# The instruction orders of a two-layer decoder kernel, chosen by another model of the framework

## The chip, the cores and the metric

The kernel runs on one core of a Trainium2 chip. The metric is the time of one execution on the device, in microseconds (us); the times given are medians of several executions. A core has engines that work side by side, each through its own list of instructions in order: PE (matmuls; PEld is its loading of weights), DVE (vector operations), ACT (activations, casts and copies), POOL, and SP, which here only issues DMAs (transfers between the device's memory and the core's own memory). An instruction that needs the result of another engine waits for it, and everything behind it on its own engine waits too.

## The reference

Two decoder layers on one sequence of 512 positions and 2048 features, in float32. Layer A is differential attention with 8 heads (two score matrices per head, values 256 wide), layer B forgetting attention with 16 heads on keys, values and forget gates that are projected once from layer A's result.

```python
for l in range(DEPTH):                                   # DEPTH = 2
    mod = c_act @ w_mod[l] + b_mod[l]                    # c_act = silu(c)
    shift, scale, gate = jnp.split(mod, 3, axis=-1)
    h = x * (1.0 + scale[:, None]) + shift[:, None]
    if l < N_A:                                          # layer A
        y = diff_attention(h, a_w_in[l], a_w_out[l], ...)
    else:                                                # layer B
        k_sh, v_sh, F_sh = shared_kv(x, c_act, kv_w_mod, kv_b_mod, kv_w, kv_b_f)
        y = forgetting_attention(h, b_w_in[l - N_A], b_w_out[l - N_A], k_sh, v_sh, F_sh)
    x = layer_norm(DN_ALPHA * x + gate[:, None] * y, ln_g[l], ln_b[l])
```

In `diff_attention`, a head's weights are softmax of its first scores less lambda times softmax of its second; the head's output is normalised by its root mean square and multiplied by `silu(g)`, before `w_out`.

## The kernel before

**Products in three parts.** Every float32 operand of a large product is split into a high part (a cast, on ACT) and a low part (the rest, on DVE), and `products` (L171) issues three matmuls: high by high, high by low, low by high. A weight tile covers 256 rows and 512 columns. `WeightStream` (L50) takes it through three steps: SP loads it (`wst`, four buffers, L46), ACT casts it (`whi`, three buffers, L93), DVE subtracts (`wlo`, three buffers, L94). For the 512 positions and one weight tile, `group` (L306) issues 24 matmuls (2 rows of tiles, 4 accumulators, 3 products).

**Stages.** The start computes layer A's shift and scale and the projections of the first two heads; its `sms` loads feed sums `sacc` on DVE (L474 to L476), which PE turns into columns (L506). Its steps follow a string (`START`, L30), and `tc.manual_schedule(engines={ET.DVE})` (L417) keeps DVE's instructions there in program order. Then layer A goes by heads: a group for values and gate (`vg[h]`, evacuated by `evac_vg`, where L675 makes `sg`) and a group for queries and keys (`qk[h]`), while the attention of the head before, cut into pieces, is put between the bursts of matmuls (`tick`, L290). A piece list ends with the tail of a head: `turn` (transposes of the weights, L720, split into `ah` and `al`), `values` (`o`, L736), `norm` (a copy and squares on ACT, L746 and L749, then sums, an inverse root and `og` on DVE, L750 to L755) and `store` (transposes of `og`, L767, and `ogT` on ACT, L769). There is one accumulator bank for `o` and one for transposes (`tr`); four for `acc`. After layer A come its output projection, the shared values and keys (`vj`, `kj`), eight pairs of heads of layer B, whose weights are turned at L1163 and split at L1166 and L1167, and the second output projection, which closes with the layer norm.

**Modulation in the background.** The other vectors of shift, scale and gate are products of one row with a matrix and are computed on DVE: `mod_stream` (L355) loads rows of the matrix (`ms`, L369) and adds them into `macc` (L384, L386). In layer A a load is 512 KB and there are two buffers; the second stream, during the projection of values and keys, has 256 KB and three. The next load into a buffer is issued when the `macc` that read it is done. A finished sum is split, summed over partitions by PE (L406, L407), and sent away (`mrow`, L408).

**What sets the order.** The program names its instructions in one sequence. The framework then sets the order in which each engine gets its own: it goes through the instructions with a model of how long each takes and takes, on each engine, an instruction that the model has ready first, so that the order on an engine may differ from the sequence. This is done for PE, ACT, DVE, SP and POOL, save DVE in the start. The model used is a simple one of the framework's own. On PE, 46 runs of instructions (440 instructions) stand outside the program's sequence.

## Time and profile before

| what | value |
|---|---|
| time, median of 3 executions | 2016.16 us (2014.56 to 2017.47) |
| time of the profiled execution | 2017.03 us |
| its span, first to last instruction | 2015.2 us |
| PE busy | 1966.7 us (98%) |
| DVE busy | 1334.4 us (66%) |
| ACT busy | 722.3 us (36%) |
| granted clock of PE, mean | 0.995 |
| moved by DMA | 353.79 MB, 176 GB/s on the mean |

The span is the profiler's; the time holds 1.8 us around it. In the page, a group of instructions is written as line, engine, operation, output<-inputs, count, then busy time and mean duration in ns, then the idle time of the engine ahead of it and what ended that. In the view of waits, a row is the waiting instruction, the one waited for, the total in us, how many times, and the longest. Lines are those of the kernel before; a line can be a helper's.

### The profile page before, as it was taken

What the parts mean: (1) busy time and instruction counts of PE and PEld (TensorE: products, weight loads), DVE (VectorE), ACT (ScalarE), POOL (GpSimd) and SP (SyncE); (2) the same over time, 40 slices, a digit from 0 to 9 for tenths busy, and PEclk for the clock granted to TensorE, in tenths of its full rate; (3) what the DMA queues carried; (4) which work ended last, traced back from release to release, by engine and by line L of the source; (5) the groups of instructions that cost most, each with busy time, mean ns of one, the idle gap of its engine ahead of it and who ended that gap; (6) DMA issues with size and microseconds to landing.
All of it is one profiled execution on the core that took longest, in us unless ns stands there. A gap on an engine that the chain in (4) does not pass through costs nothing.

```text
span 2015.2 us, 25053 instructions
## 1 busy us (share of the span) xinstructions
PE 1966.7 (98%) x9115; PEld 1624.6 (81%) x9115; DVE 1334.4 (66%) x2435; ACT 722.3 (36%) x1230; POOL 2.2 (0%) x10
## 2 busy tenths in 40 slices
PE   5999999999999999999999999999999999999997
PEld 4888878888878888888878877888888888888885
DVE  7887878777667677753575666645455555576678
ACT  2423444433333334432273222224333333453232
POOL 0000000000000000000000000000000000000000
PEclk8999999999999999999999999999999999999998
DMA  9995755574556565552344878844233323333754
GB/s 342 346 314 149 238 174 162 166 222 156 190 166 210 160 225 178 162 165 94 115 144 135 268 252 260 259 123 129 90 104 95 104 90 104 95 117 93 259 191 177
DMA packets 263095, 353.79 MB, mean 176 GB/s; under 512 B 18022, under 2 KB 162556, under 8 KB 262204
## 3 DMA queue, kind: packets, MB, share of 16 engines
q1 hardware_dynamic: 260592, 347.99, 53.7%
q10 hardware_dynamic: 2380, 4.21, 0.6%
q8 instruction: 71, 1.16, 0.2%
q14 instruction: 52, 0.43, 0.1%
HBM read 339.47 MB, written 12.66 MB: 175 GB/s over the span
## 4 chain that ended last, share of the span: by engine, by line
PE 77%; DVE 10%; DMA 10%; issue 2%; ACT 1%; SPq 1%; DVEq 0%; ACTq 0%
PE acc L173 22%; PE acc L175 22%; PE acc L174 22%; DMA ms<-in_w_mod_dram 7%; DVE macc L386 3%; DVE wlo L94 2%; PE sc L173 2%; PE sc L174 2%; PE sc L175 1%; DMA ms<-in_kv_w_mod_dram 1%; PE o L175 1%; PE o L174 1%; PE o L173 1%; PE tr L1163 1%; DMA sms<-in_w_mod_dram 1%
## 5 line engine op out<-in xcount | busy, mean ns | idle before, releaser
L93 ACT CAST whi<-wst 128x1024 fp32r<-128x1024 f32 (+2 forms) x339 | 349.5, 1032 | 672.9 <-PE acc L175 281.6
L94 DVE TENSOR_TENSOR wlo<-wst,whi 128x1024 fp32r<-128x1024 f32 (+2 forms) x339 | 404.4, 1195 | 268.1 <-ACT whi L93 263.9
L173 PE MATMUL acc<-whi,hh 128*128 128x512 f32 x1252 | 492.6, 397 | 0.9 <-ACT hh L933 0.8
L174 PE MATMUL acc<-wlo,hh 128*128 128x512 f32 x1252 | 489.7, 391 | 2.6 <-DVE wlo L94 2.6
L175 PE MATMUL acc<-whi,hl 128*128 128x512 f32 x1252 | 488.1, 390 | 0.0
L173 PE MATMUL acc<-hh,whi 128*128 128x512 f32 x1184 | 468.5, 396 | 1.3 <-ACT vt L977 0.9
L175 PE MATMUL acc<-hh,wlo 128*128 128x512 f32 x1184 | 462.3, 390 | 2.0 <-DVE wlo L94 2.0
L174 PE MATMUL acc<-hl,whi 128*128 128x512 f32 x1184 | 461.7, 390 | 0.0
L386 DVE SCALAR_TENSOR_TENSOR macc<-ms,cact,macc 128x512 f32<-128x512 f32 x360 | 269.9, 750 | 128.4 <-DMA ms<-in_w_mod_dram 95.6
L175 PEld LDWEIGHTS acc<-whi,hl 128*128 128x128 f32 x1252 | 235.3, 188 | 50.8 <-DVE hl L934 0.3
L174 PEld LDWEIGHTS acc<-wlo,hh 128*128 128x128 f32 x1252 | 235.6, 188 | 47.8 <-DVE wlo L94 4.3
L173 PEld LDWEIGHTS acc<-whi,hh 128*128 128x128 f32 x1252 | 235.7, 188 | 46.8 <-ACT hh L933 1.2
L175 PEld LDWEIGHTS acc<-hh,wlo 128*128 128x128 f32 x1184 | 222.3, 188 | 52.2 <-DVE wlo L94 4.2
L173 PEld LDWEIGHTS acc<-hh,whi 128*128 128x128 f32 x1184 | 222.5, 188 | 45.7 <-ACT vt L977 1.7
L174 PEld LDWEIGHTS acc<-hl,whi 128*128 128x128 f32 x1184 | 222.6, 188 | 41.1
L476 DVE SCALAR_TENSOR_TENSOR sacc<-sms,cact,sacc 128x512 f32<-128x512 f32 (+1 forms) x127 | 89.5, 705 | 4.8 <-DMA sms<-in_w_mod_dram 1.2
L1152 ACT ACTIVATE eb<-eb,mnb 128x128 f32<-128x128 f32 (+1 forms) x64 | 36.1, 563 | 96.4 <-DVE mnb L1149 95.2
L703 ACT ACTIVATE e<-e,mn 128x128 f32<-128x128 f32 (+3 forms) x64 | 36.0, 563 | 89.5 <-DVE mn L699 88.7
L1149 DVE CUSTOM_DVE_ANT_0 eb<-sc,biasb 128x128 f32<-128x128 f32 (+1 forms) x64 | 31.3, 490 | 52.7 <-PE sc L175 52.7
L1167 DVE TENSOR_TENSOR pTl<-tr,pTh 128x128 fp32r<-128x128 f32 (+1 forms) x64 | 31.2, 487 | 26.5 <-ACT pTh L1166 26.2
L1166 ACT CAST pTh<-tr 128x128 fp32r<-128x128 f32 (+1 forms) x64 | 27.2, 424 | 43.6 <-PE tr L1163 43.1
L769 ACT ACTIVATE ogT<-tr,subg 128x128 f32<-128x128 f32 x64 | 20.0, 364 | 56.4 <-PE tr L767 56.4
(251 smaller groups left out, 1739.2 us busy)
## 6 DMA issues: line engine op xcount, KB each, us to landing
wst<-in_a_w_in_dram SPq DMA_DIRECT2D x240, 256.0 KB
ms<-in_w_mod_dram SPq DMA_DIRECT2D x64, 512.0 KB
ms<-in_kv_w_mod_dram SPq DMA_DIRECT2D x64, 512.0 KB
wst<-in_kv_w_dram SPq DMA_DIRECT2D x64, 512.0 KB
ms<-in_w_mod_dram SPq DMA_DIRECT2D x128, 256.0 KB
wst<-in_b_w_in_dram SPq DMA_DIRECT2D x128, 256.0 KB
sms<-in_w_mod_dram SPq DMA_DIRECT2D x56, 512.0 KB
wst<-in_b_w_out_dram SPq DMA_DIRECT2D x48, 512.0 KB
```

Of the source, the lines that this page charges most:

```text
L93: self.nc.scalar.copy(hi[:, :, :w], st[:, :, :w])
L94: self.nc.vector.tensor_tensor(lo[:, :, :w], st[:, :, :w], hi[:, :, :w].bitcast(F32), op=ALU.subtract)
L173: PE.matmul(dst, lhs[0], rhs[0], start=start, stop=False)
L174: PE.matmul(dst, lhs[0], rhs[1], start=False, stop=False)
L175: PE.matmul(dst, lhs[1], rhs[0], start=False, stop=stop)
L386: V.scalar_tensor_tensor(acc, w, cact[:, kt : kt + 1], acc, op0=ALU.mult, op1=ALU.add)
L476: V.scalar_tensor_tensor(acc, w, sc, acc, op0=ALU.mult, op1=ALU.add)
L703: S.activation(e[:, :w], e[:, :w], AF.Exp, bias=mn, scale=-1.0, accum_out=rs)
L1149: V.tensor_tensor_reduce(out=e[:, :w], in0=sc[:, :w], in1=bias[:, :w], scale=-1.0, scalar=3.0e38, op0=ALU.add, op1=ALU.min, accum_out=mn)
L1152: S.activation(e[:, :w], e[:, :w], AF.Exp, bias=mn, scale=-1.0, accum_out=rs)
L1166: S.copy(pTh[:, 0 : i + 1, ts], src)
L1167: V.tensor_tensor(pTl[:, 0 : i + 1, ts], src, pTh[:, 0 : i + 1, ts].bitcast(F32), op=ALU.subtract)
```

## The change

`schedule_with_timeline_sim=True` is given to the framework's `TileContext`, by way of a small class that keeps the kernel's call as it was. With it, the pass that sets the orders takes its times from the framework's timeline simulator and not from the simpler model. The instructions themselves, their tiles and their buffers stay; nine lines are added ahead of the kernel, so that every line number of the kernel grows by 9.

```diff
-import concourse.tile as tile
+from concourse.tile import TileContext
 from concourse import mybir
...
+class tile:
+
+
+    @staticmethod
+    def TileContext(nc):
+        return TileContext(nc, schedule_with_timeline_sim=True)
+
...
 def tile_yoco(
     ctx: ExitStack,
-    tc: tile.TileContext,
+    tc: TileContext,
```

The set of instructions is the same on every engine (9068 matmuls and transposes on PE, 2437 instructions on DVE, 1095 on ACT, 1026 on SP, 15 on POOL). On PE, 369 runs of instructions (3134 instructions) now stand outside the program's sequence.

## The prediction

> **What bounds the kernel now.** I read the page's engine totals first, then PE's waits, then busy time by stretch, and after that single stretches of the timeline.

> ```profile
> span 2015.2 us, 25053 instructions
> ...
> PE 1966.7 (98%) x9115; PEld 1624.6 (81%) x9115; DVE 1334.4 (66%) x2435; ACT 722.3 (36%) x1230; POOL 2.2 (0%) x10
> ...
> L386 DVE SCALAR_TENSOR_TENSOR macc<-ms,cact,macc 128x512 f32<-128x512 f32 x360 | 269.9, 750 | 128.4 <-DMA ms<-in_w_mod_dram 95.6
> ```

> ```profile
> PE tr L506 <- DVE sacc L476: 11.4, 2, 11.0
> PE tr L767 <- DVE og L753: 4.4, 5, 1.3
> ...
> PE acc L174 <- DVE wlo L94: 2.6, 4, 1.0
> PE acc L175 <- DVE wlo L94: 2.0, 4, 0.9
> PE tr L767 <- DVE al L169: 0.9, 1, 0.9
> ...
> PE tr L720 <- DVE ss L750: 0.6, 1, 0.6
> ```

> ```profile
> 0.00:30.00 30.00, 13.37 (x67) 11.38 (x67) 19.25 (x41) 4.82 (x6) 1.60 (x9) 0.97 0.98 314
> 30.00:40.00 10.00, 7.41 (x22) 5.70 (x23) 6.94 (x11) 3.23 (x4) 0.00 (x0) 0.57 1.09 385
> ...
> 1100.00:1320.00 220.00, 214.81 (x934) 174.18 (x933) 143.32 (x179) 54.86 (x65) 0.00 (x0) 1.00 0.78 252
> 1320.00:1800.00 480.00, 480.00 (x2268) 399.47 (x2268) 269.07 (x527) 189.87 (x330) 0.00 (x0) 1.00 0.32 101
> ...
> 1950.00:2015.00 65.00, 51.20 (x224) 41.34 (x222) 55.82 (x98) 17.04 (x19) 0.00 (x0) 0.92 0.51 177
> ```

> PE's matmuls are the bound: 1966.7 of 2015.2 us. The columns of the last view are length, busy time of PE, PEld, DVE, ACT and POOL, the granted clock, the share of the DMA engines and GB/s. Of the 48.5 us in which PE is idle, 30.0 − 13.37 + 10.0 − 7.41 = 19.2 lie in the first 40 us and 65.0 − 51.20 = 13.8 at the end. Some 15.5 us are left for all the rest, and from 1320 to 1800 there is none. The instructions stay the same ones; only their order on PE, ACT, DVE and SP changes. So the most that a better order can give between 40 and 1950 us is 15.5 us, while a worse one can cost without limit: each engine takes its instructions in order, and PE stops wherever the order brings a matmul before its operand. I therefore set the new order beside the old one, instruction by instruction, and for each PE instruction that needs a result of ACT or DVE I counted the PE work that stands between the instruction that starts that result and the one that needs it. I call this the lead. Where the lead is shorter than the chain takes in the trace of before, the difference is a stall. 6343 of the 9068 matmuls and transposes change places (by up to 202), 1774 of 2437 on DVE, 692 of 1095 on ACT, 653 of 1026 on SP (by up to 16). The hand-written start keeps DVE's order alone.

> **Start: +2.5 us.**

> ```profile
> 33.82 0.94 SPq L425 DMA_DIRECT2D xt<-in_x_dram  x1
> 34.86 12.48 SPq L449 DMA_DIRECT2D sms<-in_w_mod_dram  x8
> 47.44 1.85 SPq L46 DMA_DIRECT2D wst<-in_a_w_in_dram  x2
> ```

> ```profile
> 41.38 1.02 PE L506 MATMUL tr<-ones,sacc 128*128 128x1 f32 x8 [0.37 <-DVE sacc L476]
> ```

> The new SP order puts this 1 MB `xt` load and these two 256 KB `wst` loads ahead of the `sms` loads of the next columns. At the 385 GB/s of 30 to 40 us, 1.5 MB take 4 us, and the sums on DVE that L506 waits for have no slack (0.37 us idle). A later `wst` costs nothing here: it is earlier now. Bounds 0 (later loads of `sms` are ahead again by as much) and 5; I take the middle.

> **First modulation stream, 190 to 276 us: +5.** Here the 512 KB `ms` loads have two buffers. The `macc` steps (L386) stand about six `wlo` splits (L94) earlier on DVE than before; a split behind a `macc` that waits for its load makes `acc` late. Bounds 0 and 10 (two to three loads late, priced below), middle taken.

> **Tails of the heads in layer A: +47, the largest term.** A head's last work is a chain: `turn` (L720), `ah`/`al` (L168/169), `o` (L736), the norm (L746 to L755), `tr` (L767), `ogT` (L769). Before, PE has weight products between its links. This is its price, in heads 2 to 3 (PE, then ACT, then DVE):

> ```profile
> 379.57 0.28 PE L175 MATMUL o<-vh,al 128*128 128x256 f32 x1
> 379.69 0.40 PE L173 MATMUL acc<-whi,hh 128*128 128x512 f32 x1
> 379.92 0.40 PE L174 MATMUL acc<-wlo,hh 128*128 128x512 f32 x1
> ...
> 386.51 0.38 PE L767 MATMUL tr<-ident,og 128*128 128x128 f32 x2
> ```

> ```profile
> 375.98 0.58 ACT L168 CAST ah<-tr 128x512 fp32r<-128x512 f32 x1
> ...
> 379.89 0.59 ACT L746 COPY og<-o 128x512 f32<-128x512 f32 x1 [0.80 <-PE o L175]
> ...
> 387.22 0.64 ACT L769 ACTIVATE ogT<-tr,subg 128x128 f32<-128x128 f32 x2
> ```

> ```profile
> 377.25 0.68 DVE L169 TENSOR_TENSOR al<-tr,ah 128x512 fp32r<-128x512 f32 x1
> ...
> 381.52 0.17 DVE L750 TENSOR_SCALAR ss<-ss 128x2 f32<-128x2 f32 x1 [3.59 <-ACT o L749]
> ...
> 383.98 0.88 DVE L753 SCALAR_TENSOR_TENSOR og<-og,rstd,sg 128x256 f32<-128x256 f32 x2
> ```

> The last `o` is done about 379.85; `og` is done at 384.86, some 4.6 to 5.0 us later, of which ACT's copy and squares are 1.6. PE filled these with 512-column products, 0.23 us each, and came to L767 only at 386.51: a lead of 6.8 us. The split after a transpose costs 0.58 + 0.68, about 1.3 us; `ogT`, which frees the one `tr` bank, 0.65. In the new order PE first issues all `acc` products of the group, and then this, with nothing between (the lead in us stands behind each):

> ```
> turn(0) 3.4, o 0.0, turn(1), o 0.0, turn(2), o 0.0, store(0) 1.1, turn(3) 0.0, o 0.0, store(1) 0.3, o x10, store(2) 0.0, acc of qk[3] 0.2
> ```

> The first `acc` of the next group needs `sg` (L675), which stands on DVE behind `og`. By the links: splits 0.8 + 1.0 + 1.6 (the third meets the squares of the norm, since there is one `o` bank), the rest of the first norm 1.9, `ogT` and the fourth split 0.65 + 1.3, the second norm 4.6, less 0.2 of lead: 11.6 us. On DVE more stands inside this chain:

> ```profile
> 354.81 0.75 DVE L386 SCALAR_TENSOR_TENSOR macc<-ms,cact,macc 128x512 f32<-128x512 f32 x1 [1.66 <-DMA ms<-in_kv_w_mod_dram]
> ...
> 363.11 0.75 DVE L386 SCALAR_TENSOR_TENSOR macc<-ms,cact,macc 128x512 f32<-128x512 f32 x1 [1.27 <-DMA ms<-in_kv_w_mod_dram]
> ```

> Six loads of two `macc` each stand between the first split and the first `og`, behind a `wlo` whose buffer PE frees only at the end of its `acc` products. The rows show the first `macc` of the third and of the fifth: 8.3 us for two loads, 4.15 each. With two buffers, two of the six can have landed, and the other four come in two pairs: 4.15 for the load and 1.5 for its `macc` (2 x 750 ns), twice, make 11.3; with `ogT` and the fourth split (1.95) and the second norm (4.6) about 18 us. The others, in order of time (new order beside the rows above): heads 3 to 4 a norm less 0.4, 4.2, and with four loads inside one such pair more (5.65 + 4.6), about 10.5; 4 to 5 a split and a norm, 5.9; 5 to 6 a norm and `ogT`'s turn, 4.9; 6 to 7 part of a norm and an `ogT`, 2.8, and 6.5 with the `macc` and `wlo` inside; 7 to the output projection a split, a norm, two `ogT` and the `hh` split, 7.5. Sum 53, by the links alone 37. Before's own stalls at these places go: 4.4 + 0.9 + 0.6 = 5.9 in the waits above. That leaves +47 with the loads and +31 without; I take 47, since the loads stand in the order that DVE has to follow. Bounds 31 and 60.

> **Second modulation stream, 1100 to 1317 us: +14.**

> ```profile
> DVE macc L386 <- DMA ms<-in_w_mod_dram: 72.5, 49, 3.6
> ```

> ```profile
> L369 SPq DMA_DIRECT2D ms<-in_w_mod_dram x127: 327/328/1771, 1096.4 to 1311.4; - x127
> ```

> ```profile
> 1295.58 1.22 DVE L94 TENSOR_TENSOR wlo<-wst,whi 128x1024 fp32r<-128x1024 f32 x1
> ...
> 1315.94 0.75 DVE L386 SCALAR_TENSOR_TENSOR macc<-ms,cact,macc 128x512 f32<-128x512 f32 x1
> ```

> 127 loads take 215 us, one in 1.71 us: with three buffers, each is issued when a `macc` ends, and DVE waits 72.5 us for them. This pace does not depend on the order. The new order sets each `wlo` behind more of these `macc`: the one that ran at 1295.58 now stands behind the one that ran at 1315.94, 12 further on. Counted in `wlo`, the last `macc` have 212 of them ahead and not 215. Three weight pairs are 3 × 24 products × 0.227 = 16.3 us of PE work, of which the `wlo` had 1 to 3 us to spare (PE waited up to 1.0 us for it, four times at each of two lines). So PE ends the stream 14 us later, and there is nothing behind it that makes this good, as PE is full to 1800. Bounds 8 (a spare of one and a half pairs) and 18.

> **End of layer B, 1845 to 1870 us: +5.5.** Four of the splits of `pTh`/`pTl` (L1166, L1167) and the `hh` split of the last heads follow their transposes with leads of 0 to 0.7; at the 1.3 us of a 512-column split, less what is narrower. Bounds 2 and 8.

> **The clock: +5.**

> ```profile
> 29.00:34.00 5.00, 1.41 (x5) 1.01 (x6) 2.45 (x5) 1.85 (x3) 0.00 (x0) 0.50 1.10 378
> 34.00:38.00 4.00, 4.00 (x10) 3.13 (x10) 3.54 (x5) 0.33 (x2) 0.00 (x0) 0.50 1.09 386
> ...
> 39.00:40.00 1.00, 1.00 (x6) 0.81 (x5) 0.96 (x2) 0.04 (x1) 0.00 (x0) 1.00 1.05 407
> ```

> Around 29 to 34 us PE has little to do, and the granted clock is half until past 38, although from 34 on PE is full: some 4.8 us of products at half speed, 2.4 us lost. The tails leave gaps of 4 us and more at six places. I take two such losses; bounds 0 and 14 (six). [...]

> **Gains: −2.** From 1400 to 1800 us the leads grow a great deal, but there PE has nothing to gain (480.00 of 480.00). Of the rest, some stalls between 248 and 273 us go. Bounds 0 and −7.5, all that is left of 15.5 after the 5.9 above and 2 that stay.

> **Sum.** 2.5 + 5 + 47 + 14 + 5.5 + 5 − 2 = +77. The profiled execution took 2017.0 us (its span and 1.8 us around it), 0.9 above the median of the three runs, 2016.2. So the forecast is 2093 us for a median. All low ends together give 0 + 0 + 31 + 8 + 2 + 0 − 7.5 = +33.5, 2050; the high ones 5 + 10 + 60 + 18 + 8 + 14 = +115, 2131. The prices are of one kind and can all be off in one direction, so the range is 2040 to 2140.

> **The rivals.**
> - The loads have landed when the tails come (links only, and `wlo` keeps its spare): 31 + 8 and the rest at their middle, without the clock, +50, 2066 us. For it: DVE is busy for only 66% of the span. Against: two buffers hold two loads, and more than two stand inside two of the chains.
> - All six gaps drop the clock: +9 on the sum, 2102; with the high ends 2131. For it: the stretch at 29 us. Against: it is one place, and the weak stretch there was longer than 4.6 us.
> - Faster: the longer leads outside the tails take away the 15.5 us of stalls in the middle, about 2004 us; with only half of it 2009. It would need the tail's chain to lie beside products after all, and the point at which that decides is a lead of about 4.6 us between the last `o` and its L767. Before has 6.8 there and the new order 0.0, so PE would have to come late to that place for another reason, and then time is lost already.
> - The change does nothing: excluded, since the orders differ; only an order that differs where PE has slack everywhere would give 2016.

> **How the numbers follow.** My sum with its loads inside (2075 to 2115) 0.5; links only 0.25; all clock drops or high ends 0.15; not slower 0.10, of which faster 0.07 and within 0.2% 0.03. About 0.2% (4 us) is what a measurement of this kernel can tell from no change. From 2040 to 2140 leaves out the not slower and a little beyond the top, under 2 in 10. Slower: 0.90.

> **What would show it.** Right: PE's waits of the changed kernel list L767's transposes on `og` and the next group's `acc` on `sg` (now lines 776 and 684) with some 30 us or more; PE's busy share in 300 to 900 us falls to about 93%; DVE waits for `ms` within the tails; the last `macc` of the second stream comes before the same number of `acc`, with PE waiting for `wlo` (line 103) 10 us and more; the granted clock shows stretches of 0.5 at tails. Wrong: a PE without gaps at 380 to 400, and `macc` that end ahead of the tails. I would be most wrong if PE's idle time were not at the tails but shared out over the whole of layer A, which would mean that leads are not what counts.

## The result, and the profile after

The changed kernel takes 2157.35 us (median; 2153.30 to 2159.07), the kernel before 2016.82 in the same series: a ratio of 1.0691, 95% interval 1.0667 to 1.0715. That is 140 us slower, where 2093 us had been forecast, in a range up to 2140. The sign was right, the size was not. The profiled execution has a span of 2155.3 us and a mean granted clock of 0.968.

The page of the changed kernel (its line numbers are 9 above those of before):

```profile
span 2155.3 us, 25058 instructions
...
PE 2011.1 (93%) x9115; PEld 1653.6 (77%) x9115; DVE 1327.8 (62%) x2435; ACT 716.0 (33%) x1230; POOL 2.1 (0%) x10
...
PEclk9999999799898999998999999999999999999998
```

Its PE waits (total, times, longest):

```profile
PE tr L776 <- DVE og L762: 48.6, 7, 12.7
PE tr L515 <- DVE sacc L485: 13.7, 2, 11.1
PE acc L184 <- DVE wlo L103: 9.5, 7, 3.5
PE acc L183 <- DVE wlo L103: 6.6, 4, 4.4
```

And busy time by stretch (length, busy PE, PEld, DVE, ACT, POOL, granted clock, DMA share, GB/s):

```profile
40.00:200.00 160.00, 145.46 (x667) 118.45 (x665) 117.73 (x165) 53.16 (x72) 0.56 (x1) 0.96 0.76 257
...
300.00:600.00 300.00, 265.54 (x1200) 217.78 (x1200) 184.42 (x400) 98.75 (x210) 0.00 (x0) 0.91 0.47 149
600.00:900.00 300.00, 275.00 (x1258) 227.36 (x1257) 189.83 (x394) 97.28 (x200) 0.00 (x0) 0.95 0.52 165
...
1320.00:1400.00 80.00, 71.37 (x295) 56.43 (x294) 49.54 (x64) 18.05 (x22) 0.00 (x0) 0.96 0.74 240
1400.00:1800.00 400.00, 396.32 (x1841) 329.35 (x1840) 207.64 (x383) 143.16 (x236) 0.00 (x0) 1.00 0.34 109
```

PE is idle for 2155.3 − 2011.1 = 144.2 us, 95.7 more than before. The other 44.4 us are in its busy time: the same matmuls took longer, in good part at a lower granted clock (0.968 in the mean and not 0.995), as the clock row shows. The transposes L776 wait 48.6 us for `og` where they waited 4.4, and `wlo` costs 16.1 us where it cost 4.6. Those are the places that the prediction named. Its sign for them, a busy share of about 93% from 300 to 900 us, came out as 88.5% and 91.7%; of the other waits that it named, those of the next group's `acc` for `sg`, there is only 0.6 us.

To see where the time came from, I gave each matmul its time at full clock and asked of both traces when PE has done the same amount of this work. The lateness of the changed kernel grows so:

```
stage (time before, us)              forecast   measured
start, 0 to 94                           2.5        4.6
94 to 218 (forecast: 190 to 276)         5         19.5
218 to 377                              -2         -5.8
tails of layer A, 377 to 909        47 + 5         92.7
909 to 1166                              0          1.6
second modulation stream, to 1325       14         16.0
layer B, to 1785                         0         -0.2
end of layer B, to 1908                  5.5        7.2
second output projection and end         0          4.5
sum                                     77        140.1
```

The 5 is the clock, which the forecast did not divide among the stages. Four terms lie within their bounds. Two do not: the tails, off by 41 us, and 94 to 218 us, off by 14.5. Of the 19.5 us there, 17 had arisen by 190 us, ahead of the stretch that the forecast named.

**A tail of layer A.** The last `o` of head 2 and the next transposes, on PE, ACT and DVE of the changed kernel:

```profile
427.52 0.41 PE L184 MATMUL o<-vh,al 128*128 128x256 f32 x1
434.01 0.66 PE L776 MATMUL tr<-ident,og 128*128 128x128 f32 x2 [6.08 <-DVE og L762]
434.77 0.80 PE L182 MATMUL acc<-hh,whi 128*128 128x512 f32 x1
```

```profile
427.97 0.59 ACT L755 COPY og<-o 128x512 f32<-128x512 f32 x1 [1.51 <-PE o L184]
428.45 1.21 ACT L177 CAST vh<-acc 128x256 fp32r<-128x256 f32 x4
429.51 0.43 ACT L758 ACTIVATE o<-o 128x256 f32<-128x256 f32 x1
...
429.90 0.69 ACT L683 ACTIVATE th<-acc 128x256 f32<-128x256 f32 x2
430.43 0.43 ACT L758 ACTIVATE o<-o 128x256 f32<-128x256 f32 x1
```

```profile
428.87 1.42 DVE L178 TENSOR_TENSOR vl<-acc,vh 128x256 fp32r<-128x256 f32 x4 [3.81 <-ACT vh L177]
431.01 0.17 DVE L759 TENSOR_SCALAR ss<-ss 128x2 f32<-128x2 f32 x1 [0.72 <-ACT o L758]
...
433.38 0.88 DVE L762 SCALAR_TENSOR_TENSOR og<-og,rstd,sg 128x256 f32<-128x256 f32 x2
```

PE does nothing for 6.08 us. The norm was priced at 4.6 from the rows of before; here four casts `vh` and two `th` stand on ACT between the copy and the last square, so that copy and squares take 2.9 us (427.97 to 430.86) and not 1.6. Four `vl` stand on DVE ahead of `ss` too, but are done before the last square. At heads 3 to 4, `macc` stand inside the norm too:

```profile
545.58 0.75 DVE L395 SCALAR_TENSOR_TENSOR macc<-ms,cact,macc 128x512 f32<-128x512 f32 x1 [1.25 <-DMA ms<-in_kv_w_mod_dram]
...
548.27 0.75 DVE L395 SCALAR_TENSOR_TENSOR macc<-ms,cact,macc 128x512 f32<-128x512 f32 x1 [1.09 <-DMA ms<-in_kv_w_mod_dram]
```

```profile
550.36 0.66 PE L776 MATMUL tr<-ident,og 128*128 128x128 f32 x2 [12.65 <-DVE og L762]
```

Only 1.25 + 1.09 of the 12.65 us are waits for loads; eight `macc` between `ss` and `og`, the first a shorter one, are another 5.7 (0.48 + 7 x 0.75). The gaps of the six tails, in order, are 20.6 (in ten pieces), 12.7, 10.1, 6.1, 8.5 and 8.5 us: 66.4 where 53 had been forecast, and each of the six is longer than its forecast.

**The clock.** Behind the tail above:

```profile
428.00:434.00 6.00, 0.00 (x0) 0.02 (x1) 4.03 (x19) 2.98 (x11) 0.00 (x0) 0.50 0.00 0
434.00:437.00 3.00, 2.89 (x7) 2.10 (x8) 1.77 (x5) 1.17 (x4) 0.00 (x0) 0.50 0.02 5
437.00:441.00 4.00, 4.00 (x12) 3.06 (x11) 0.00 (x0) 0.00 (x0) 0.00 (x0) 0.56 0.00 0
441.00:443.00 2.00, 2.00 (x11) 1.65 (x10) 0.00 (x0) 0.63 (x2) 0.00 (x0) 1.00 0.00 0
```

PE is full again from 434, at half speed until about 440 (12 matmuls in 4 us, then 11 in 2). The clock had been at half since about 407 us, through all the gaps between the pieces of this tail. The trace shows 15 such stretches of work at half speed between 44 and 1393 us, in 11 falls of the clock, with 27.6 us lost by the measure above, 1.8 for each stretch; 18 of it at the tails. These are the six tails (the granted clock is the third number from the right):

```profile
400.00:443.00 43.00, 22.35 (x79) 16.68 (x78) 24.31 (x66) 10.87 (x33) 0.00 (x0) 0.60 0.38 119
530.00:560.00 30.00, 17.23 (x73) 13.48 (x72) 19.52 (x43) 7.94 (x23) 0.00 (x0) 0.72 0.46 142
648.00:672.00 24.00, 13.78 (x55) 10.66 (x54) 11.58 (x30) 6.96 (x21) 0.00 (x0) 0.72 0.31 102
760.00:778.00 18.00, 11.73 (x51) 9.40 (x51) 7.02 (x24) 5.88 (x19) 0.00 (x0) 0.81 0.19 60
868.00:888.00 20.00, 11.49 (x47) 8.67 (x46) 14.35 (x36) 6.76 (x21) 0.00 (x0) 0.74 0.48 150
970.00:1000.00 30.00, 21.51 (x85) 16.01 (x84) 14.22 (x35) 8.11 (x20) 0.00 (x0) 0.77 0.53 154
```

### The profile page after: what moved, and what is told of

It reads as the page before. It is cut to its first block, busy times and chain, and to the rows that moved or that the text cites. A ratio compares the mean times of both kernels' runs of the same rounds, so it can differ in the third digit from the quotient of the medians.

```text
span 2155.3 us, 25058 instructions
## 1 busy us (share of the span) xinstructions
PE 2011.1 (93%) x9115; PEld 1653.6 (77%) x9115; DVE 1327.8 (62%) x2435; ACT 716.0 (33%) x1230; POOL 2.1 (0%) x10
## 4 chain that ended last, share of the span: by engine, by line
PE 73%; DMA 13%; DVE 9%; issue 2%; ACT 2%; SPq 1%; DVEq 0%; ACTq 0%
PE acc L182 21%; PE acc L183 20%; PE acc L184 20%; DMA ms<-in_w_mod_dram 8%; DMA ms<-in_kv_w_mod_dram 3%; DVE macc L395 3%; DVE wlo L103 2%; PE sc L182 2%; PE sc L184 2%; PE sc L183 2%; PE o L184 1%; PE o L182 1%; PE o L183 1%; PE tr L1172 1%; DMA sms<-in_w_mod_dram 1%
## 5 line engine op out<-in xcount | busy, mean ns | idle before, releaser
L182 PE MATMUL acc<-whi,hh 128*128 128x512 f32 x1252 | 480.9, 397 | 3.8 <-ACT hh L177 1.8
L184 PE MATMUL acc<-whi,hl 128*128 128x512 f32 x1252 | 480.8, 392 | 0.0
L183 PE MATMUL acc<-hl,whi 128*128 128x512 f32 x1184 | 468.7, 396 | 0.0
L776 PE MATMUL tr<-ident,og 128*128 128x128 f32 x64 | 15.2, 326 | 53.8 <-DVE og L762 48.6
L776 PEld LDWEIGHTS tr<-ident,og 128*128 128x128 f32 x64 | 8.8, 160 | 59.9 <-issue 51.1
```

The costliest lines, as they stand in the source:

```text
L182: PE.matmul(dst, lhs[0], rhs[0], start=start, stop=False)
L183: PE.matmul(dst, lhs[0], rhs[1], start=False, stop=False)
L184: PE.matmul(dst, lhs[1], rhs[0], start=False, stop=stop)
L776: PE.transpose(pt[:, e * P : (e + 1) * P], og[:, i % 2, e * P : (e + 1) * P], ident)
```

## The experiments

Time is that of the kernel named; the kernel before took 2014.9 to 2019.0 us in these series. Lateness is against the kernel before, by the measure above.

**Whose order: PE's or DVE's.** First by the program's own sequence in layer A. `a_pe` is this diff; `a_dve` has `ET.DVE`:

```diff
+    hand0 = ExitStack()
+    hand0.enter_context(tc.manual_schedule(engines={ET.PE}))
     load_parameters()
...
+    hand0.close()
     npool, n, nstats = zp
```

> The changed kernel with PE's instructions of layer A, from the second head to the output projection, kept in the program's sequence; DVE, ACT and SP stay with the new model. Theory 1 (the cost of layer A is PE's order: the tails stand bare): the 92 us by which PE falls behind over the six boundaries go, 2157 becomes 2055 to 2080. Rival (it is DVE's order, with loads inside the norm, whatever PE does): PE still waits for og, no more than 30 us come back, 2125 or more.

> The changed kernel with DVE's instructions of layer A kept in the program's sequence; PE, ACT and SP stay with the new model. Theory 1: the tails stay bare on PE and still cost about 6 us of norm each, only the loads inside go: 20 to 30 us less than 2157, 2127 to 2137. Rival (DVE's order is the cause): 60 us or more less, below 2097.

`a_pe` took 2131.3 us, the rival's number, and `a_dve` 2176.7, which neither gave. In `a_pe` the tails from heads 2 to 3 on add 33 us and not 92, as theory 1 has it, but the first heads add 28 us more than in the changed kernel. I put that down to the other engines' orders, which the new model set around another order of PE; no run shows it. In `a_dve`, 38 us arise at the last tail alone. The program's sequence is not the old order, so I held engines to the very order of the kernel before, by edges that only fix who is issued first (`PE_ORDER_OF_BEFORE` stands here for the packed list of names):

```diff
+def pin(tc, packed):
...
+    order = zlib.decompress(base64.b64decode(packed)).decode().split()
+    made = {i.name: i for i in tc.nc.cur_bb.bb.instructions}
+    order = [n for n in order if "I-" + n in made]
+    for first, then in zip(order, order[1:]):
+        tc.add_manual_dep(
+            made["I-" + then], "I-" + first,
+            mybir.DependencyInfo(mybir.DependencyClass.NoSync, mybir.DependencyReason.DATA), reason="pin",
+        )
...
         tile_yoco(tc, *args)
+        pin(tc, PE_ORDER_OF_BEFORE)
```

> The changed kernel with PE held to the order that it has in the kernel before, all through; DVE, ACT and SP are ordered by the new model around it. Theory 2 (after a_pe: DVE's order costs as much as PE's, since the new model sets it for waits that the chip does not have): not more than 40 us come back, 2115 to 2150. Theory 1 (PE's order alone; a_pe missed it since the program's sequence is not the old order): 2030 to 2080.

> The changed kernel with DVE, ACT and SP held to the orders that they have in the kernel before; PE alone is ordered by the new model. Theory 1: the tails stay bare on PE and cost their links, 6 us of norm each and half clock: 2090 to 2130. Theory 2 (the loss is in DVE's and ACT's orders): 2020 to 2050.

`pe_old` took 2098.4 us, `others_old` 2207.1. PE's waits between 250 and 1000 us, `pe_old` and then `others_old`:

```profile
PE tr L789 <- DVE og L775: 14.4, 6, 4.5
```

```profile
PE tr L789 <- DVE og L775: 32.0, 5, 8.8
PE tr L789 <- DVE mrow L430: 11.9, 2, 6.4
```

From 250 us to the end of the tails the lateness grows by 32 us with PE's old order (14 to 46) and by 99 with PE's new one among the old orders of the rest (13 to 111); in the changed kernel it grows by 88. So giving PE its old order back takes away about two thirds of the loss in layer A, and giving the others theirs takes away none. The last third is not split further: in `pe_old` the new model set DVE's and ACT's orders around PE's old one. In the second stream it is the other way round: 18 us with PE's old order (54 to 73), 2 with the old orders of the others (121 to 123). Neither theory's bounds were met: PE's order is the larger part, but no engine's order alone is the cause. `others_old` loses another 58 us in and behind layer B, where the changed kernel loses 7; my reading, which no run tests, is that the new model there set PE around orders that it would not have chosen.

**The loads.** All four engines were held to the orders of the changed kernel, and each modulation load made an eighth:

```diff
+        few = slice(0, 64)
...
-            nc.sync.dma_start(t, rows.rearrange("(k p) n -> p k n", p=P) if nk > 1 else rows)
+            nc.sync.dma_start(t[:, :, few] if nk > 1 else t[:, few], (rows.rearrange("(k p) n -> p k n", p=P) if nk > 1 else rows)[..., few])
...
-                w = t[:, kk, :] if nk > 1 else t
+                w = (t[:, kk : kk + 1, few] if nk > 1 else t[:, few].rearrange("p (o n) -> p o n", o=1)).broadcast_to([P, 8, 64])
...
```

> All four orders held to those of the changed kernel; each modulation load (both streams) brings 64 of its 512 columns, which macc reads eight times over, so that the sums in the background are not the right ones, DVE's work is the same and the loads are an eighth. If the loads inside the chains are what lengthens them, heads 2 to 3 lose 6 to 10 us of gap and 3 to 4 about 6 (and half clock), the second stream 12 to 16: 2115 to 2130. If they are not, within 5 us of 2157.

2115.5 us, as expected in sum. Its wait for `og`, over the whole span:

```profile
PE tr L791 <- DVE og L777: 43.8, 7, 10.2
```

By this wait alone the loads were worth 5 us in the tails (48.6 to 43.8; the long gap 12.65 to 10.2). But PE also waits less for `al`, earlier in the tails: the gaps of the six tails sum to 57.8 us and not 66.4, and with the half clock behind them the lateness grows by 78 us from 377 to 909 us and not by 92. So the loads were worth 8.6 us in gaps and 14 in time there. In the second stream no wait of PE is left at all, and the 16 us turn into a gain of 8 against the kernel before: without the slow loads nothing is lost there. (SP issues the loads of the weights too; whether these came sooner beside an eighth of the modulation loads, I have not told apart.)

> The changed kernel with PE, ACT and SP, besides DVE, kept in the program's sequence in the start, and DVE in the second modulation stream (from the shared values and keys to layer B). If the 24 us of the first 240 us are the orders of PE, ACT and SP in the start and the 16 us of the second stream are DVE's, 30 to 40 us come back: 2117 to 2127, with no change between. If the start's loss is the first stream behind it (from 190 us), only 16 to 22: 2135 to 2141.

The edit adds PE, ACT and SP to the `manual_schedule` of the start and opens one for DVE from `npool, n, nstats = zp` to `load_pair(0)`. 2149.3 us, outside both ranges. The second stream again lost nothing (lateness 130 to 122), here with the loads as they were: its 16 us need both the slow loads and DVE's new order. In the start, the program's sequence made things worse, 41 us late at 218 us instead of 24. With PE's old order it was 10, of which 5 arose behind 94 us; with the old orders of the others 12, nearly all of it behind 94 us. So PE's order carries most of the loss there, and the waits are of this kind (changed kernel, 100 to 245 us):

```profile
PE sc L184 <- DVE wlo L103: 3.6, 2, 2.2
PE sc L182 <- ACT hh L530: 3.2, 3, 1.2
PE sc L182 <- DVE part L565: 2.1, 1, 2.1
PE tr L246 <- DVE lam L241: 1.8, 1, 1.8
PE acc L182 <- DVE part L565: 1.8, 1, 1.8
```

**The clock.** On `a_pe`, where PE's order is written by hand, the tails can be laid bare on purpose. The edit puts twelve empty pieces ahead of the fourth `turn`, so that the last pieces of each head run after all products of the next group. As there is one buffer for a head's values, these late pieces read the next head's; the amount of work is the same.

```diff
-            values(2), store(0), turn(3), store(1), values(3), None, None, None, None, store(2), store(3),
+            values(2), store(0), *[None] * 12, turn(3), store(1), values(3), None, None, None, None, store(2), store(3),
```

> As a_pe, but the last pieces of each head (the fourth turn, the last o, the last two stores) are put off until all products of the next group are issued, so that eight tails stand bare in PE's order. Theory 1: each tail adds a split (1.3), a norm (5 to 6), an ogT (0.7) and some 2.5 of half clock, about 10 us, 80 us for eight: about 2145. Rival (bare tails matter only with modulation loads inside): 1 to 3 us each, below 2090.

2210.5 us: 79 more than `a_pe`, as eight bare tails of 10 us give (the 2145 that was expected counted on a faster `a_pe`). PE's waits of L776 grow from 19.6 to 63.4 us for `og` and from 4.5 to 22.6 for `al`. This is the clearest evidence that a bare tail costs this much. `a_pe_late_fill` and `late_full_fill` cover the gaps with products that nothing uses (the second is shown):

```diff
+                spare = sc_bank() if i in (1, 2) else None
+                for _ in range({1: 14, 2: 24}.get(i, 0)):
+                    PE.matmul(spare, ones_a, cur[h, "k0"][0], start=True, stop=True)
                 pt = tr_bank()
                 og = st["og", i // 2]
...
```

> As a_pe_late, with 16 more 512-column products into the free transpose bank between the last o and the first store of the last two (3.6 us of PE work that nothing uses, in each of eight tails). Theory of the clock (the gap itself costs, and then again as half clock behind it): the granted clock stays at 1.0 behind the tails, and the time falls by 15 to 25 us against a_pe_late although PE has 29 us more to do. Rival (a gap costs its length alone): the same time as a_pe_late within 4 us, or longer.

> As a_pe_late, with 14 unused 512-column products (3.2 us) ahead of the second store of a head and 24 (5.4 us) ahead of the third, into a free bank for scores, so that nearly the whole of each late tail is covered. As in a_pe_late, the late pieces read the next head's values, so the attention is not the right one. Theory of the clock: with the gaps covered the half clock behind the tails goes, the 23 us that it costs in layer A more than before (35 against 12 of excess over full speed) fall to below 10, and the time is 15 us or more below a_pe_late, 2195 or less, with 69 us of products more. Rival (the half clock does not come from the gaps): the excess stays at 30 or more, and the time is 2202 or more.

With part of one gap covered: 2202.1 us, 8 less. PE's matmuls in layer A took as much over full speed as before (38 and 39 us), while the granted clock of the whole run rose from 0.964 to 0.973, so that neither theory was met; the tails' other gap, 4.3 us ahead of the second store, was still open. With both covered: 2200.3 us. `a_pe_late` and then `late_full_fill`, 250 to 1060 us:

```profile
250.00:1060.00 810.00, 701.64 (x3140) 575.31 (x3139) 480.60 (x1017) 258.93 (x529) 0.00 (x0) 0.93 0.47 150
```

```profile
250.00:1060.00 810.00, 763.09 (x3493) 627.19 (x3492) 483.29 (x1019) 261.26 (x531) 0.00 (x0) 0.98 0.48 151
```

The granted clock rises from 0.93 to 0.98, and the excess over full speed falls from 38 to 26 us. The tail at 455 to 470 us, `a_pe_late` and then `late_full_fill`:

```profile
455.00:470.00 15.00, 8.69 (x33) 6.90 (x34) 8.55 (x28) 5.45 (x18) 0.00 (x0) 0.77 0.01 1
```

```profile
455.00:470.00 15.00, 13.53 (x62) 10.81 (x61) 9.47 (x19) 4.51 (x9) 0.00 (x0) 1.00 0.28 88
```

Where this tail is covered, the half clock behind it is gone (1.00 here, where it was 0.77). From 250 to 1060 us PE is still idle for 46.9 us. 304 unused products (8 x 38) added nothing to the time. So here the half clock went where the gaps went. The time and the excess lie between what the two theories gave: 12 us went, and 14 more than in the kernel before (12) stayed; my reading is that they stayed since not every gap was covered.

**The length of the bare norm.** Two edits with all orders of the changed kernel held, but for the one named: on ACT the squares moved directly behind their copy; on DVE 31 `macc` moved from inside the norms to behind `og`. Both change only the list given to `pin`.

> All four orders held to those of the changed kernel, but on ACT the two squares of each norm stand directly behind their copy of o, ahead of the casts and tanh of the group's accumulators. If these casts and tanh (1.10 + 0.55 us between copy and last square) are why the bare norm costs PE 6.08 us and not the 4.6 of the prediction, the six gaps shrink to about 4.5 us each and the time falls by 8 to 13 us, 2144 to 2149. If the norm is longer for another reason: within 4 us of 2157.

> All four orders held to those of the changed kernel, but on DVE the 31 macc that stand between the first step of a norm and its og are put behind the og. If these macc and their loads are what makes 12.65 us of the gap at heads 3 to 4 (and 7.39 at 6 to 7), those gaps become 6 to 6.5 us, and the time falls by 8 to 14 us, 2143 to 2149. If the time only moves to later waits for the same loads: within 4 us of 2157.

Neither shortened the kernel. `act_squares` took 2160.5 us, within 4 us of the changed kernel as its rival has it, and this gap is 6.25 us: DVE takes `ss` only behind the four `vl`, and these wait for the casts, which now come later.

```profile
428.93 1.19 ACT L190 CAST vh<-acc 128x256 fp32r<-128x256 f32 x4
```

```profile
429.33 1.42 DVE L191 TENSOR_TENSOR vl<-acc,vh 128x256 fp32r<-128x256 f32 x4 [4.76 <-ACT vh L190]
430.66 0.15 DVE L772 TENSOR_SCALAR ss<-ss 128x2 f32<-128x2 f32 x1
```

`og_first` took 2170.0, which neither side gave. The wait for `og` falls to 5.83, and the first `acc` behind it then waits for `sg`, which now stands behind the `macc`:

```profile
543.42 0.66 PE L789 MATMUL tr<-ident,og 128*128 128x128 f32 x2 [5.83 <-DVE og L775]
553.02 0.80 PE L195 MATMUL acc<-hh,whi 128*128 128x512 f32 x1 [8.94 <-DVE sg L697]
```

With PE's order bare, what stands on DVE between the last `o` and the last `sg` was in the way in both runs, in whatever order it stood.

**A version that beats both.** In the second stream the kernel before stood 5.2 us. Three kernels on its simpler model: DVE in the program's sequence there (`b_kv_hand`); five `ms` buffers and four loads ahead (`b_ms5`); and four buffers with three loads ahead, with that sequence (`b_ms5_kv_hand`, whose label says five, though it has four).

```diff
-        ahead = 2 // nk
+        ahead = 1 if nk > 1 else 4
...
-        lambda: npool.tile([P, 512], F32, name="ms", tag="ms", bufs=3),
+        lambda: npool.tile([P, 512], F32, name="ms", tag="ms", bufs=5),
```

> The kernel before with its own simpler model, but DVE kept in the program's sequence from the shared values and keys to layer B. In start_kv_hand the second stream ended 8 us earlier against PE's work than in the changed kernel at its start, and 3.5 us earlier than before. If that is DVE's order: 2 to 5 us less than before. If it came from PE's new order: no change, within 2 us.

> The kernel before with five buffers in place of three for the 256 KB loads of the second stream, and four loads ahead in place of two. If the 5.2 us in which PE stands between 1100 and 1320 us come from the wait for these loads: 3 to 5 us less, and DVE's 72.5 us of waiting for ms fall below 20. If they come from the weight loads that share the queue: no change or longer.

> The kernel before with four buffers and three loads ahead in the second stream, and DVE in the program's sequence there. Both together cannot give more than the 5.2 us of idle PE: 2 to 5 us less than before.

`b_ms5` took 2009.2 us, a ratio to the kernel before of 0.9961 (0.9947 to 0.9976); `b_kv_hand` 2010.1, 0.9965 (0.9954 to 0.9977); `b_ms5_kv_hand` 2011.0, 0.9972 (0.9961 to 0.9984). All beat both kernels, the one before by 6 to 8 us, where at most 5 had been expected, and the two edits do not add up. DVE's wait for the loads between 1100 and 1320 us was 72.5 us; in `b_kv_hand` and in `b_ms5` (for which below 20 had been expected) it is

```profile
DVE macc L386 <- DMA ms<-in_w_mod_dram: 19.8, 18, 3.1
```

```profile
DVE macc L386 <- DMA ms<-in_w_mod_dram: 24.7, 24, 3.2
```

and PE is idle for 0.0 us there in both. The gain is larger than the idle time removed, 5.2: the matmuls of that stretch also come closer together. Before, 934 of them fill 214.81 us, 0.230 each; in both new kernels 970 fill 220.00, 0.227 each. That is another 3 us, and 8 together, by which PE is earlier behind the stretch. The two do it in opposite ways, as the loads of the stream show, `b_kv_hand` and then `b_ms5`:

```profile
L369 SPq DMA_DIRECT2D ms<-in_w_mod_dram x128: 327/328/1486, 1092.0 to 1349.8; - x128
```

```profile
L369 SPq DMA_DIRECT2D ms<-in_w_mod_dram x128: 327/328/2345, 1083.0 to 1279.2; - x128
```

The program's sequence spreads the 128 loads over 258 us, so that most have landed when their `macc` comes; more buffers let them run ahead and be done in 196. Before it was 219 us.

## Why the prediction was wrong

The forecast was 77 us of 140. By its own steps:

- **The place and the cause of the tails: right.** Bare tails in PE's order wait for `og` (48.6 us of waits). `a_pe_late` makes them on purpose and pays 10 us each; `pe_old` takes two thirds of the loss away.
- **The tail term (+47): mis-sized.** The gaps are 66.4 us, less before's 5.9, where 53 less 5.9 had stood. The step that failed is pricing the norm at 4.6 us by the rows of before: those show ACT and DVE free at that place, and in the new order their queues hold the casts, `vl` and `macc` that stand between. The same norm left PE idle for 6.08 us at three tails where no `macc` stands in it, and for 12.65 where eight do. The loads in the chain, argued at 16 us, were worth 8.6 in gaps. What was priced too low is the rest, the links: 57.8 us of gaps stay without the loads, where 37 had been forecast.
- **The clock (+5): the step that failed most.** The price of one drop was about right (2.4 forecast; 27.6 us over 11 falls is 2.5, over 15 stretches 1.8), but two drops were taken, as an estimate, and there were 11, with 27.6 us. Its bounds (0 to 14) assumed one loss for each of six tails at the most. Behind 44 us PE has nine gaps of 3.49 to 12.65 us, and the granted clock was 0.50 to 0.56 in the 2.5 us behind each; for four of them it had fallen before they began (at 406, 656 and 976 us). Shorter gaps went both ways: behind a pair of them (1.84 and 2.08 us at 196 and 198 us) it was 0.50 from 200 to 205 us, and it fell at 137 us, where the longest gap in the 10 us before was 0.87 us, while behind single ones of 2.25 to 2.45 us (at 173, 1334 and 1419 us) it was 1.00.
- **94 to 218 us (+5): 19.5.** The term was for the `macc` behind 190 us; the 17 us ahead of that had no term at all, that is, they were put at nothing without a reason. The hand-written start fixes DVE only, and PE's new order in it, with half clock behind its waits (a granted clock of 0.96 from 40 to 200 us), was not screened. With PE's old order 5 us of the 19.5 are left.
- **The second stream (+14): right**, 16.0, and by the cause named: `wlo` behind `macc` that wait for loads (`thin_loads` and `start_kv_hand` each take one of the two away, and no wait is left). The pace of the loads, said not to depend on the order, is the same in the changed kernel (218.8 us from the first issue to the last, as before), but `b_kv_hand` shows that an order can set a slower one (257.8 us).
- **Start, end of layer B, gains** (2.5, 5.5, −2): 4.6, 7.2 and −5.8, all within their bounds.
- **A remainder.** The 95.7 us of idle time and the 27.6 us of the clock do not make up the whole of the 140: some 17 us of PE's longer busy time lie outside both. They may be small matmuls at half speed and the ends of matmuls ahead of gaps; I have not told these apart. The 27.6 is a low count: PE is busy for 70 us within the 11 falls of the clock, and half of that is 35.

The range ended at 2140 because all upper bounds came from rows of a run in which PE hardly stood behind its start; how its gaps would feed the clock was bounded by the tails that I had listed, not by the gaps that could occur.

## What to carry to other kernels

When an order changes on all engines, price a chain by what now stands in the queues of the engines that it passes through, not by its links in a run where they were free; moving one thing in such a queue only moved the wait here (`act_squares`, `og_first`). Count the gaps of the matmul engine, not just their length: here each of the nine of 3.49 to 12.65 us had half clock behind it, and a stretch of that cost 1.8 us in the mean. A background stream that waits for loads on the engine that also prepares the weights should have buffers enough, or an order, that never let it stand ahead of them: that was worth 6 to 8 us in a kernel that seemed full.
